# Strided attention: normalised weights, turned over by TensorE, in place of raw exponentials and a division at the exit

## Chip, cores and metric

One core of a Trainium2 chip. The metric is the device time of one execution in microseconds; a kernel's time is the median of its runs. The profile of one execution gives, beside that, the span from the first to the last instruction and what every engine did in it.

## The reference

Every query attends to the same 16 positions, every 64th of 1024. There are 8 x 12 = 96 heads with 64 dimensions, all in float32:

```python
for i in range(seq):
    attend_positions = np.arange(0, seq, stride)          # 0, 64, ..., 960
    q = Q[:, :, i:i + 1, :]
    k = K[:, :, attend_positions, :]
    v = V[:, :, attend_positions, :]
    scores = np.einsum('bhqd,bhkd->bhqk', q, k) * scale   # scale = 1/8
    weights = np.exp(scores - np.max(scores, axis=-1, keepdims=True))
    weights = weights / (np.sum(weights, axis=-1, keepdims=True) + 1e-10)
    result[:, :, i, :] = np.einsum('bhqk,bhkd->bhqd', weights, v)[:, :, 0, :]
```

## The kernel before, in words

The 96 heads are 24 groups (`NG`) of 4 heads. A group's queries are 1 MB of float32 and lie in SBUF as 128 partitions of 2048 elements: a partition holds 32 queries of one head, 64 dimensions each. Ten buffers `qn` take the loads, eight `out_sb` the stores. All DMAs go through the SP queue: the first ten loads of Q (and K's and V's rows) at the start, then one load and one store a group. The last groups' stores go in pairs, and the very last store has its own place at the end.

For each group the steps are these:

- `cast` (L326): Q to bf16 in `qb`, one half by ScalarE (ACT), one half by GpSimd (POOL).
- `transpose` (L337): VectorE (DVE) turns 32x32 blocks of pairs of bf16 (as int32), so that the dimensions lie on partitions, in `qt`.
- `scores` (L343, products in L463 to 477): TensorE (PE) multiplies four times, 512 columns wide, the keys `k_t` as the stationary operand and the queries as the moving one. The scores come out with the keys (head and position) on partitions and the queries along the columns, in one PSUM bank `sc`.
- two exponentials by ScalarE (L353), 64 partitions each, from PSUM straight into the block matrix `w_all`. No maximum is subtracted.
- `outputs` (L367): eight products `w x v_all`, 260 columns wide, in blocks of 3, 2 and 3, into two PSUM tiles `o` of three banks. `v_all` carries the values in a block diagonal (made by POOL, `values`, L316) and four columns of ones, whose products are the sums of the weights.
- the exit: for each block VectorE takes the reciprocal of the sums (L453); for the first two blocks it multiplies the outputs by it from PSUM into `out_sb` (L459); the third block is copied by ScalarE (L383) and multiplied by POOL in SBUF (L385).

The order on each engine is written out by hand. `Program.op` records the operations in order with what they read and write, `plan` works out which waits are needed, and `emit` writes the instructions; every engine carries out its own in the order recorded. PE and VectorE run loops (`pe_stream`, `dve_stream`: four groups a turn on PE, eight on VectorE); ScalarE, POOL and SP are written out straight. Semaphores named "gates" (`turned`, `raised`, `scaled`, `copied`, ...) tell the loops how far the other engines are. Scores run one group ahead of the outputs, casts and transposes two or three.

Of the kernel before, what the change touches and what calls it, by code (L numbers as in the profile page):

```python
# [42 lines left out]
class Program:  # L43
# [13 lines left out]
    def op(self, engine, fn, reads=(), writes=(), after=(), lane=None, gate=None, gates=(), looped=False, last=False):  # L57
# [12 lines left out]
        for k in writes:  # L70
# [3 lines left out]
            gate=gate, gates=gates, last=last, looped=looped or engine == "PE",  # L74
# [3 lines left out]
    def plan(self):  # L78
# [12 lines left out]
        for i, o in enumerate(self.ops):  # L91
# [4 lines left out]
            for d in sorted(o["deps"], reverse=True):  # L96
                p = self.ops[d]
                if p["lane"] == e and (e == "PE" or d not in o["own"]):
                    continue
                if known[e].get(p["lane"], -1) >= d:  # L100
                    continue
                assert not o["looped"], ("needs more gates", i, e, d, p["lane"])
                while d is not None and self.ops[d]["gate"]:
                    later = (j for j in range(d + 1, i) if self.ops[j]["lane"] == p["lane"])
                    d = next(later, None)
                if d is None:
                    d = self.ops.index(p)
                    gate_waits.append((p["gate"], carriers[p["gate"]].index(d) + 1))
                else:
                    waits.append(d)  # L110
                learn(e, d)
# [22 lines left out]
    def emit(self, loops):  # L134
# [8 lines left out]
        with self.tc.tile_critical(no_gpsimd_drain=True):  # L143
            for e in ("ACT", "DVE", "POOL"):
                engines[e].addr_align(128, max_nops=0)
            for o in self.ops:
                if o["looped"]:
                    continue
                for gate, n in o["gates"]:
                    engines[o["engine"]].wait_ge(gates[gate], n)  # L150
# [8 lines left out]
            nc.sync.wait_ge(sems["POOL"], counts["POOL"])  # L159
            for loop in loops:  # L160
                loop(sems, gates)
# [5 lines left out]
def kernel(  # L167
# [19 lines left out]
    KW = P + NK  # L187
    TURN = 4
    ROUNDS = 8
    assert B * H == NG * HG and S == 1024 and D == 64 and NK == 16 and NG % TURN == NG % ROUNDS == 0  # L190
# [6 lines left out]
    edge = sb.tile([P, 32], FP32, name="edge")  # L197
    k_raw = sb.tile([P, NC, D], FP32, name="k_raw")
    v_raw = sb.tile([P, NC, D], FP32, name="v_raw")
    k_bf = sb.tile([P, NC, D], BF16, name="k_bf")  # L200
    identity = sb.tile([P, P], BF16, name="identity")
    qn = [sb.tile([P, 32 * D], FP32, name=f"qn{i}") for i in range(QBUFS)]
    qb = [sb.tile([P, 32 * D], BF16, name=f"qb{i}") for i in range(2)]
    out_all = [sb.tile([P, 2, 4, 8, D], FP32, name=f"out_sb{i}") for i in range(OBUFS // 2)]
    out_sb = [out_all[i // 2][:, i % 2] for i in range(OBUFS)]
    qt = [sb.tile([P, 32 * D], BF16, name=f"qt{i}") for i in range(2)]
    rec = [sb.tile([P, 8, 4], FP32, name=f"rec{i}") for i in range(2)]
    w_all = sb.tile([P, 2, 8, P], BF16, name="w_all")
    v_all = sb.tile([P, 4, 4 * D + 4], BF16, name="v_all")
    w_bufs, v_bufs = [w_all[:, i] for i in range(2)], [v_all[:, i] for i in range(4)]  # L210
    k_t = sb.tile([P, NG + 1, 2, KW], BF16, name="k_t")
    k_r = sb.tile([P, NC, D], BF16, name="k_r")
    v_bf = sb.tile([P, NC, D], BF16, name="v_bf")
    v_rep = sb.tile([P, NC, 2, D], BF16, name="v_rep")
    perm_v = sb.tile([P, 2, 2, 2, 2, NK], BF16, name="perm_v")
    s_sel = sb.tile([P, 4], BF16, name="s_sel")
    mask = sb.tile([P, 4, D], BF16, name="mask")
    sc_ps = [ps.tile([P, 512], FP32, name=f"sc{i}") for i in range(2)]
    o_ps = [ps.tile([P, 3, 512], FP32, name=f"o{i}") for i in range(2)]
# [4 lines left out]
    blocks = ((0, 3), (3, 2), (5, 3))  # L224
# [19 lines left out]

    op("POOL", lambda: nc.gpsimd.memset(identity, 0.0), writes=["identity"])
# [5 lines left out]
    for c in range(2):  # L251
        for a in range(2):
            op("POOL", lambda c=c, a=a: nc.gpsimd.tensor_copy(
                out=perm_v[:, c, a],
                in_=id_v[:, c, :, a].unsqueeze(2).to_broadcast([P, 2, 2, NK]),
            ), reads=["identity"], writes=[f"perm{c}{a}"])
    op("DVE", lambda: nc.vector.memset(k_t, 0.0),  # L257
       writes=[f"k_t{m}{c}{s}" for m in range(2) for c in range(2) for s in range(4)],
       gate="scaled")
    op("DVE", lambda: nc.vector.memset(w_all, 0.0),  # L260
       writes=[f"w{i}{a}" for i in range(2) for a in range(2)], gate="scaled")
# [5 lines left out]
        out=v_all[:, :, 4 * D :], in_=s_sel.unsqueeze(1).to_broadcast([P, 4, 4])  # L267
    ), reads=["s_sel"], writes=["ones"])
    op("POOL", lambda: nc.gpsimd.tensor_copy(
        out=mask, in_=s_sel.unsqueeze(2).to_broadcast([P, 4, D])  # L270
    ), reads=["s_sel"], writes=["mask"])

# [11 lines left out]
    def keys(m, c, s):  # L284
        part = halves[m]
        src, dst, col = 32 * (2 * c + s % 2), 32 * (2 * (s % 2) + s // 2), NK + 32 * s
        e, fn = (
            ("DVE", nc.vector.tensor_copy) if m else
            ("POOL", nc.gpsimd.tensor_copy) if s >= 2 else ("ACT", nc.scalar.copy)
        )  # L290
        op(e, lambda: fn(  # L291
# [3 lines left out]
            )[:, s // 2],  # L295
        ), reads=[f"k_r{m}"] + ["mask", "turn"] * (e == "POOL"),
           writes=[f"k_t{m}{c}{s}"] + ["turn"] * (e == "POOL"), gate="copied" if (m, c, s) == (0, 1, 1) else None)

    def value_sums(n):
        rows = o_ps[n][:, 0:2, 0 : NC // 2 * D].rearrange("p c (n d) -> p c n d", d=D)  # L300
        for c in range(2):
            r = nc.tensor.matmul(  # L302
                rows[:, c], lhsT=perm_v[:, c].rearrange("p a b e k -> p (a b e k)"),
                rhs=v_bf[:, 6 * n : 6 * n + 6], start=True, stop=True,
            )
        return r

    def value_rows(n):
        op("PE", None, reads=["v_bf"] + [f"perm{c}{a}" for c in range(2) for a in range(2)],
           writes=[f"o{n}"], gates=[("masked", 1)], gate="out")  # L310
        rows = o_ps[n][:, 0:2, 0 : NC // 2 * D].rearrange("p c (n d) -> p c n d", d=D)
        op("DVE", lambda: nc.vector.tensor_copy(  # L312
            out=v_rep[:, 6 * n : 6 * n + 6].rearrange("p n c d -> p c n d"), in_=rows
        ), reads=[f"o{n}"], writes=[f"v_rep{n}"], gates=[("out", n + 1)])

    def values(g):  # L316
        v = v_bufs[g % 4]
        op("POOL", lambda: nc.gpsimd.tensor_tensor(  # L318
            out=v[:, 0 : 4 * D].rearrange("p (s d) -> p s d", s=4), in0=mask,
            in1=v_rep[:, g // 2, g % 2].unsqueeze(1).to_broadcast([P, 4, D]),  # L320
            op=ALU.mult,
        ), reads=["mask", "v_rep0", "v_rep1"], writes=[f"v{g % 4}"], gate="masked")

    half = 16 * D

    def cast(g):  # L326
        q, b = qn[g % QBUFS], qb[g % 2]
        op("ACT", lambda: nc.scalar.copy(b[:, half:], q[:, half:]),  # L328
           reads=[f"qn{g % QBUFS}1"], writes=[f"qb{g % 2}1"])
        op("POOL", lambda: nc.gpsimd.tensor_copy(out=b[:, 0:half], in_=q[:, 0:half]),  # L330
           reads=[f"qn{g % QBUFS}0"] + [f"qb{g % 2}1"] * (g >= 2) + ["turn"] * (g < 2),
           writes=[f"qb{g % 2}0"] + ["turn"] * (g < 2), gate="cast")

    def turn_over(g):
        return nc.vector.transpose(qt[g % 2].bitcast(I32), qb[g % 2].bitcast(I32))  # L335

    def transpose(g):  # L337
        k_in = {0: "00", 1: "01"}.get(g)
        op("DVE", lambda: turn_over(g),
           reads=[f"qb{g % 2}0", f"qb{g % 2}1"] + [f"k_t{k_in}{s}" for s in range(4) if k_in],  # L340
           writes=[f"qt{g % 2}"], gate="turned", gates=[("cast", g + 1)], looped=g >= 2)

    def scores(g):  # L343
        s = g % 2
        op("PE", None,
           reads=[f"qt{g % 2}"] + [f"k_t{int(min(g, NG - 1) >= 8)}{g % 2}{i}" for i in range(4)],
           writes=[f"sc{s}0", f"sc{s}1"], gates=[("turned", g + 1)])
        if g == NG:
            return
        sc, w = sc_ps[s], w_bufs[g % 2]  # L350
        for a in range(2):
            wa = w[64 * a : 64 * a + 64]
            op("ACT", lambda a=a, wa=wa: nc.scalar.activation(  # L353
                out=_ap_with(wa, [wa.ap[0], [P, 8], [1, 2], [2, 32]], extra_offset=64 * a),
                in_=sc[64 * a : 64 * a + 64].rearrange("p (t x q) -> p t x q", t=8, x=2),
                func=AF.Exp, bias=0.0, scale=scale,
            ), reads=[f"sc{s}{a}"], writes=[f"w{g % 2}{a}"], gate="raised" if a else None,
               after=[stored[g - OBUFS]] if a and g >= OBUFS else [])

    def parts(g, c):  # L360
        i0, n = blocks[c]
        r = rec[g % 2][:, i0 : i0 + n]
        o = o_ps[(3 * g + c) % 2][:, 0:n, 0 : 4 * D].rearrange("p i (s d) -> p i s d", s=4)
        to = out_sb[g % OBUFS][:, :, i0 : i0 + n].rearrange("p s i d -> p i s d")
        return r, o, to, r.unsqueeze(3).to_broadcast([P, n, 4, D])

# [180 lines left out]
```

## Time and profile before

| what | value |
|---|---|
| time, median of 3 runs | 127.56 us (127.49, 127.56, 128.0) |
| span of the profiled execution | 125.9 us; its own time is not listed apart, the three runs are 1.6 to 2.1 us longer than this span |
| busy: PE, DVE, ACT, POOL | 66.5, 90.7, 80.9, 78.2 us |
| DMA | 51.15 MB, mean 406 GB/s |
| chain that ended last | DMA 25%, PE 20%, DVE 20%, ACT 13%, POOL 8% |

A row of the profile names the line of the kernel, the engine and the operation, what is written and read, the shape and the count; behind the first bar stand the busy time in us and the mean duration of one in ns, behind the second the idle time of the engine just before, and what ended it. PEld is the loading of TensorE's stationary operand. PEclk is the granted clock of TensorE, in tenths of full speed for each of 40 slices of the span.

### The profile page before, as it was taken

What the parts mean: (1) busy time and instruction counts of PE and PEld (TensorE: products, weight loads), DVE (VectorE), ACT (ScalarE), POOL (GpSimd) and SP (SyncE); (2) the same over time, 40 slices, a digit from 0 to 9 for tenths busy, and PEclk for the clock granted to TensorE, in tenths of its full rate; (3) what the DMA queues carried; (4) which work ended last, traced back from release to release, by engine and by line L of the source; (5) the groups of instructions that cost most, each with busy time, mean ns of one, the idle gap of its engine ahead of it and who ended that gap; (6) DMA issues with size and microseconds to landing.
All of it is one profiled execution on the core that took longest, in us unless ns stands there. A gap on an engine that the chain in (4) does not pass through costs nothing.

```text
span 125.9 us, 1283 instructions
## 1 busy us (share of the span) xinstructions
PE 66.5 (53%) x296; PEld 29.7 (24%) x296; DVE 90.7 (72%) x161; ACT 80.9 (64%) x103; POOL 78.2 (62%) x89
## 2 busy tenths in 40 slices
PE   0005472887777796466555666478664663840000
PEld 0001130343333333233212333233332320410000
DVE  2996457978669669989997999966999794970000
ACT  4270943686966786989999799968698655711000
POOL 4074247387865956988999699986699851534000
PEclk9999999755685559999999999955999999755555
DMA  1999989899899999899798998999998999999991
GB/s 43 423 312 479 479 354 500 354 479 448 344 417 458 403 435 495 359 474 469 338 515 354 411 515 341 430 458 398 440 482 364 450 427 422 422 422 422 424 424 70
DMA packets 7140, 51.15 MB, mean 406 GB/s; under 512 B 3808, under 2 KB 3808, under 8 KB 3808
## 3 DMA queue, kind: packets, MB, share of 16 engines
q1 hardware_dynamic: 7136, 51.12, 96.9%
q14 instruction: 4, 0.03, 0.1%
HBM read 25.95 MB, written 25.17 MB: 406 GB/s over the span
## 4 chain that ended last, share of the span: by engine, by line
DMA 25%; PE 20%; DVE 20%; ACT 13%; POOL 8%; issue 4%; SPq 1%; ACTq 0%; DVEq 0%; POOLq 0%
DMA out_dram<-out_sb 18%; DVE out_sb L459 12%; PE o L497 10%; PE sc L469 10%; DMA qn<-in_Q_dram 7%; ACT w_all L353 5%; ACT out_sb L383 4%; DVE qt L335 4%; POOL out_sb L385 4%; ACT qb L328 3%; DVE rec L453 3%; POOL qb L330 2%; DVE v_rep L312 1%; POOL v_all L318 1%; SPq L236 1%
## 5 line engine op out<-in xcount | busy, mean ns | idle before, releaser
L497 PE MATMUL o<-v_all,w_all 128*128 128x260 bf16 x192 | 38.8, 327 | 28.5 <-DVE out_sb L459 24.2
L385 POOL TENSOR_TENSOR out_sb<-out_sb,rec 128x768 f32<-128x768 f32 x24 | 35.3, 1472 | 25.3 <-ACT out_sb L383 25.3
L469 PE MATMUL sc<-qt,k_t 128*128 128x512 bf16 x100 | 33.3, 464 | 16.5 <-DVE qt L335 12.3
L459 DVE TENSOR_TENSOR out_sb<-o,rec 128x768 f32<-128x768 f32 (+1 forms) x48 | 39.6, 825 | 1.6
L353 ACT ACTIVATE w_all<-sc 64x512 bf16<-64x512 f32 x48 | 35.2, 733 | 7.3 <-DMA out_dram<-out_sb 3.5
L335 DVE STREAM_TRANSPOSE qt<-qb 128x1024 int32<-128x1024 int32 x26 | 31.6, 1214 | 3.6 <-POOL qb L330 3.5
L497 PEld LDWEIGHTS o<-v_all,w_all 128*128 128x128 bf16 x192 | 18.3, 112 | 52.4 <-DVE out_sb L459 33.0
L383 ACT COPY out_sb<-o 128x768 f32<-128x768 f32 x24 | 19.2, 799 | 16.5 <-DVE rec L453 16.2
L328 ACT CAST qb<-qn 128x1024 bf16<-128x1024 f32 x24 | 25.0, 1045 | 4.3 <-DVE v_rep L312 1.4
L330 POOL CAST qb<-qn 128x1024 bf16<-128x1024 f32 x24 | 24.9, 1039 | 1.9 <-DMA qn<-in_Q_dram 1.7
L453 DVE RECIPROCAL rec<-o 128x12 f32<-128x12 f32 (+1 forms) x72 | 15.4, 213 | 11.7 <-PE o L497 10.9
L318 POOL TENSOR_TENSOR v_all<-mask,v_rep 128x256 bf16<-128x256 bf16 x24 | 16.0, 670 | 4.2 <-DVE v_rep L312 4.1
L469 PEld LDWEIGHTS sc<-qt,k_t 128*128 (+1 forms) x100 | 10.9, 110 | 27.7 <-issue 11.7
L257 DVE MEMSET k_t<- 128x3600 uint32 x1 | 3.1, 3058 | 2.3 <-issue 2.3
L312 DVE CAST v_rep<-o 128x768 bf16<-128x768 f32 x2 | 1.9, 939 | 2.6 <-PE o L302 2.6
L291 DVE COPY k_t<-k_r 32x256 bf16<-32x256 bf16 x8 | 3.2, 395 | 0.1
L277 ACT CAST k_bf<-k_raw 128x256 bf16<-128x256 f32 (+1 forms) x2 | 0.9, 508 | 2.6 <-DMA k_raw<-in_K_dram 2.6
L266 POOL COPY v_all<-s_sel 128x16 bf16<-128x16 bf16 x1 | 0.2, 197 | 3.7 <-DVE s_sel L262 3.7
L277 ACT ACT_TABLE_LOAD x1 | 1.3, 1283 | 1.3 <-SPq L143 1.3
L302 PE MATMUL o<-v_bf,perm_v 128*128 128x384 bf16 x4 | 1.5, 520 | 1.0 <-POOL v_bf L416 1.0
L291 ACT COPY k_t<-k_r 32x128 bf16<-32x128 bf16 x4 | 1.2, 295 | 0.8 <-DVE k_r L279 0.7
L291 POOL COPY k_t<-k_r 32x128 bf16<-32x128 bf16 x4 | 1.2, 290 | 0.3
(13 smaller groups left out, 5.1 us busy)
## 6 DMA issues: line engine op xcount, KB each, us to landing
qn<-in_Q_dram SPq DMA_DIRECT2D x24, 1024.0 KB, 15.4
out_dram<-out_sb SPq DMA_DIRECT2D x16, 1024.0 KB, 14.0
out_dram<-out_sb SPq DMA_DIRECT2D x4, 2048.0 KB, 17.4
k_raw<-in_K_dram SPq DMA_DIRECT2D x1, 384.0 KB, 4.2
v_raw<-in_V_dram SPq DMA_DIRECT2D x1, 384.0 KB, 6.7
```

The lines of the kernel that those rows point to most:

```text
L291: op(e, lambda: fn(k_t[dst : dst + 32, 2 * part.start + c : 2 * part.stop : 2, :, col : col + NK], k_r[src : src + 32, part].rearrange("p ...
L318: op("POOL", lambda: nc.gpsimd.tensor_tensor(out=v[:, 0 : 4 * D].rearrange("p (s d) -> p s d", s=4), in0=mask, in1=v_rep[:, g // 2, g % 2] ...
L328: op("ACT", lambda: nc.scalar.copy(b[:, half:], q[:, half:]), reads=[f"qn{g % QBUFS}1"], writes=[f"qb{g % 2}1"])
L330: op("POOL", lambda: nc.gpsimd.tensor_copy(out=b[:, 0:half], in_=q[:, 0:half]), reads=[f"qn{g % QBUFS}0"] + [f"qb{g % 2}1"] * (g >= 2) + [ ...
L335: return nc.vector.transpose(qt[g % 2].bitcast(I32), qb[g % 2].bitcast(I32))
L353: op("ACT", lambda a=a, wa=wa: nc.scalar.activation(out=_ap_with(wa, [wa.ap[0], [P, 8], [1, 2], [2, 32]], extra_offset=64 * a), in_=sc[64 ...
L383: op("ACT", lambda: nc.scalar.copy(to, o), reads=[o_key], writes=[to_key, f"copy{g}"], after=[sums])
L385: op("POOL", lambda: nc.gpsimd.tensor_tensor(out=to, in0=to, in1=by, op=ALU.mult), reads=[to_key, r_key], writes=[to_key], last=g == NG - 1)
L453: sums = dve.reciprocal(r, o_ps[(3 * j + c) % 2][:, 0 : blocks[c][1], 4 * D : 4 * D + 4])
L459: dve.tensor_tensor(out=to, in0=o, in1=by, op=ALU.mult).then_inc(gates["scaled"], 1)
L469: r = pe.matmul(sc_ps[g % 2], lhsT=k_t[:, k, f, NK * (1 - e) : NK * (1 - e) + P], rhs=_ap_with(qt[g % 2], [qt[g % 2].ap[0], [D, 8], [16 * ...
L497: r = pe.matmul(o_ps[(3 * j + c) % 2][:, i, 0 : 4 * D + 4], lhsT=w_bufs[j % 2][:, i0 + i], rhs=v_bufs[j % 4], start=True, stop=True,)
```

## The change

The scores change sides. The queries in `qt` become the stationary operand (16 loads of 128 columns a group) and the keys the moving one (64 columns), so that the scores stand with 128 queries on partitions and 32 x 16 (query block and head part, position) along the columns of one PSUM bank. For this the transpose stores its words with a stride.

Then the softmax is made in full before the outputs:

- `largest`: VectorE takes the maximum over 16 positions from PSUM and subtracts it from the scores (PSUM to SBUF, 512 elements, `low`, one buffer).
- `raise_`: one exponential by ScalarE, 128 partitions x 512, SBUF to SBUF, float32.
- `sums`: VectorE adds over 16 positions and takes the reciprocal (32 elements).
- `weights`: POOL multiplies the exponentials by the reciprocal, into bf16 `wt`.
- `turn`: TensorE turns `wt` over, four 128 x 128 products with the identity, into a bf16 PSUM tile `tp`.
- `spread`: ScalarE copies `tp` in two halves of 64 partitions into the block matrix `wb`.
- `outputs`: eight products of 256 columns, in two halves of two PSUM banks each; there are no ones in `v_all` any more, and `v_all` is kept for all 24 groups, made for two groups at a time by POOL.
- `evict`: ScalarE copies each half, 128 x 1024 float32, from PSUM to `out_sb`; VectorE and POOL have no part in the exit. The evictions of a group are recorded in the next group's turn, one ahead of its spread copies and one behind.

From the fourth group on the cast is POOL's alone, 128 x 2048 at once. Scores and transposes now run two groups ahead, casts three. PE's loop has two groups a turn and leaves the last two groups to straight code; VectorE's loop is gone and its instructions are written out. The second half of the keys' copies moves into groups 1 to 4. The load of group g+9 and the store of group g-1 are issued in the turn of group g, behind the second eviction of g-1.

The core of the diff:

```diff
+    def score_products(g, k):
+        for i in range(8):
+            for f in range(2):
+                r = nc.tensor.matmul(
+                    _ap_with(
+                        sc_ps[g % 2], [sc_ps[g % 2].ap[0], [64, 2], [1, 32]],
+                        extra_offset=128 * (i // 2) + 32 * (i % 2),
+                    ),
+                    lhsT=_ap_with(qt[g % 2], [qt[g % 2].ap[0], [2, P]], extra_offset=2 * P * i + f),
+                    rhs=k_t[:, k, f], start=f == 0, stop=f == 1,
+                )
+        return r
...
+    def largest(g):
+        s = sc_ps[g % 2].rearrange("p (t k) -> p t k", k=NK)
+        m = top[g % 2]
+        op("DVE", lambda: nc.vector.tensor_reduce(
+            out=m, in_=s, op=ALU.max, axis=mybir.AxisListType.X,
+        ), reads=[f"sc{g % 2}"], writes=[f"top{g % 2}"])
+        op("DVE", lambda: nc.vector.tensor_tensor(
+            out=low, in0=s, in1=m.unsqueeze(2).to_broadcast([P, 32, NK]), op=ALU.subtract,
+        ), reads=[f"sc{g % 2}", f"top{g % 2}"], writes=["low"])
+
+    def raise_(g):
+        op("ACT", lambda: nc.scalar.activation(
+            out=ex[g % 2], in_=low, func=AF.Exp, bias=0.0, scale=scale,
+        ), reads=["low"], writes=[f"ex{g % 2}"])
+
+    def sums(g):
+        t, r = total[g % 2], rec[g % 2]
+        op("DVE", lambda: nc.vector.tensor_reduce(
+            out=t, in_=ex[g % 2], op=ALU.add, axis=mybir.AxisListType.X,
+        ), reads=[f"ex{g % 2}"], writes=[f"total{g % 2}"])
+        op("DVE", lambda: nc.vector.reciprocal(r, t),
+           reads=[f"total{g % 2}"], writes=[f"rec{g % 2}"])
+
+    def weights(g):
+        op("POOL", lambda: nc.gpsimd.tensor_tensor(
+            out=wt[g % 2], in0=ex[g % 2],
+            in1=rec[g % 2].unsqueeze(2).to_broadcast([P, 32, NK]), op=ALU.mult,
+        ), reads=[f"ex{g % 2}", f"rec{g % 2}"], writes=[f"wt{g % 2}"], gate="weighted")
+
+    def turn_products(g):
+        for c in range(4):
+            r = nc.tensor.transpose(
+                tp_ps[:, 2 * c : 2 * c + 2].rearrange("p a b -> p (a b)"),
+                wt[g % 2][:, 8 * c : 8 * c + 8].rearrange("p t k -> p (t k)"), identity,
             )
         return r
...
+    def spread(g):
         for a in range(2):
+            rows = slice(64 * a, 64 * a + 64)
+            op("ACT", lambda rows=rows: nc.scalar.copy(wb[g % 2][rows, :, rows], tp_ps[rows]),
+               reads=[f"tp{a}"], writes=[f"wb{g % 2}{a}"], gate="copied" if a else None)
...
+    def evict(g, n):
+        to = out_sb[g % OBUFS].rearrange("p b (c x) d -> p c b (x d)", c=4)[:, 2 * n : 2 * n + 2]
+        op("ACT", lambda: nc.scalar.copy(
+            to, o_ps[:, 2 * n : 2 * n + 2].rearrange("p c (b x) -> p c b x", b=2),
+        ), reads=[f"o{n}"], writes=[f"out{g % OBUFS}{n}"],
+           after=[stored[g - OBUFS]] if g >= OBUFS else [], last=g == NG - 1 and n == 1)
+        if n and g + 1 < NG:
+            op("ACT", lambda: nc.scalar.nop(), reads=[f"out{g % OBUFS}{n}"], gate="freed")
...
     for g in range(NG):
+        looped = g < looped_groups
+        largest(g)
+        raise_(g)
+        if g + 2 < NG:
+            transpose(g + 2)
+        sums(g)
         if g + 3 < NG:
+            cast(g + 3, False)
...
+        weights(g)
+        if g % 2 == 0 and g // 2 + 1 < NC:
+            values(g // 2 + 1)
         if g + 2 < NG:
+            scores(g + 2, looped)
+        if g >= 1:
+            evict(g - 1, 0)
+        turn(g, looped)
+        spread(g)
+        if g >= 1:
+            evict(g - 1, 1)
...
+        outputs(g, 0, looped)
+        outputs(g, 1, looped)
+    evict(NG - 1, 0)
+    evict(NG - 1, 1)
...
+        with pe.Fori(0, looped_groups // TURN) as turn_:
             for j in range(TURN):
+                pe.wait_ge(gates["turned"], j + 3)
+                score_products(j, turn_ * TURN + (j + 2)).then_inc(done, 1)
+                pe.wait_ge(gates["weighted"], j + 1)
+                turn_products(j).then_inc(done, 1)
+                pe.wait_ge(gates["copied"], j + 1)
+                output_products(j, turn_ * TURN + j, 0).then_inc(done, 1)
+                pe.wait_ge(gates["freed"], j + 1)
+                output_products(j, turn_ * TURN + j, 1).then_inc(done, 1)
```

More of the change, by code (lines that the diff above doesn't have):

```diff
@@ L266 @@
     op("POOL", lambda: nc.gpsimd.tensor_copy(
-        out=v_all[:, :, 4 * D :], in_=s_sel.unsqueeze(1).to_broadcast([P, 4, 4])
-    ), reads=["s_sel"], writes=["ones"])
-    op("POOL", lambda: nc.gpsimd.tensor_copy(
         out=mask, in_=s_sel.unsqueeze(2).to_broadcast([P, 4, D])
     ), reads=["s_sel"], writes=["mask"])
+    op("DVE", lambda: nc.vector.memset(wb_all, 0.0),
+       writes=[f"wb{i}{a}" for i in range(2) for a in range(2)])
     halves = (slice(0, 4), slice(4, NC))
@@ L282, in key_rows, with keys @@
         ), reads=[f"k_bf{m}"], writes=[f"k_r{m}"])
-    def keys(m, c, s):
+    def keys(m, c, h, engine):
         part = halves[m]
[L286 to L291, printed above, removed]
+        src, dst = 32 * (2 * c + h // 2), 32 * h
+        col = 32 * (h % 2) + NK * (h // 2)
+        fn = {
+            "DVE": nc.vector.tensor_copy, "POOL": nc.gpsimd.tensor_copy, "ACT": nc.scalar.copy,
+        }[engine]
+        op(engine, lambda: fn(
             k_t[dst : dst + 32, 2 * part.start + c : 2 * part.stop : 2, :, col : col + NK],
@@ L308, in value_rows @@
[L308 to L350, printed above, removed]
-        for a in range(2):
[L352 to L358, printed above, removed]
@@ new lines, in keys, with value_rows, products @@
+            )[:, h % 2],
+        ), reads=[f"k_r{m}"], writes=[f"k_t{m}{c}{h}"])
+    def value_rows(n):
+        rows = o_ps[:, 2 * n : 2 * n + 2, 0 : NC // 2 * D].rearrange("p c (n d) -> p c n d", d=D)
+        def products():
+            for c in range(2):
+                r = nc.tensor.matmul(
+                    rows[:, c], lhsT=perm_v[:, c].rearrange("p a i b k -> p (a i b k)"),
+                    rhs=v_bf[:, 6 * n : 6 * n + 6], start=True, stop=True,
+                )
+            return r
+        op("PE", products, reads=["v_bf"] + [f"perm{c}{a}" for c in range(2) for a in range(2)],
+           writes=[f"o{n}"], gates=[("values", 1)])
+        op("DVE", lambda: nc.vector.tensor_copy(
+            out=v_rep[:, 6 * n : 6 * n + 6].rearrange("p n c d -> p c n d"), in_=rows
+        ), reads=[f"o{n}"], writes=[f"v_rep{n}"])
@@ new lines, in values, with cast @@
+    def values(n):
+        op("POOL", lambda: nc.gpsimd.tensor_tensor(
+            out=v_all[:, 2 * n : 2 * n + 2].rearrange("p c (s d) -> p c s d", s=4),
+            in0=mask.unsqueeze(1).to_broadcast([P, 2, 4, D]),
+            in1=v_rep[:, n].unsqueeze(2).to_broadcast([P, 2, 4, D]),
+            op=ALU.mult,
+        ), reads=["mask", f"v_rep{n // 6}"], writes=[f"v{n}"])
+    half = 16 * D
+    def cast(g, shared):
+        q, b = qn[g % QBUFS], qb[g % 2]
+        if shared:
+            op("ACT", lambda: nc.scalar.copy(b[:, half:], q[:, half:]),
+               reads=[f"qn{g % QBUFS}1"], writes=[f"qb{g % 2}1"])
+            op("POOL", lambda: nc.gpsimd.tensor_copy(out=b[:, 0:half], in_=q[:, 0:half]),
+               reads=[f"qn{g % QBUFS}0"], writes=[f"qb{g % 2}0"])
+        else:
+            op("POOL", lambda: nc.gpsimd.tensor_copy(out=b, in_=q),
+               reads=[f"qn{g % QBUFS}{h}" for h in range(2)],
+               writes=[f"qb{g % 2}{h}" for h in range(2)])
@@ L398, in store @@
         sent = op("SP", lambda: send(g, n), lane=f"out{g % OBUFS}",
-                  reads=[f"out{i % OBUFS}{c}" for i in both for c in range(3)])
+                  reads=[f"out{i % OBUFS}{c}" for i in both for c in range(2)])
         stored.update((i, sent) for i in both)
@@ L403 @@
     key_rows(1)
-    for s in range(4):
-        keys(0, 0, s)
-    for s in range(4):
-        keys(1, 0, s)
-    cast(0)
-    transpose(0)
-    for s in range(4):
-        keys(0, 1, s)
-    for s in range(4):
-        keys(1, 1, s)
-    scores(0)
-    cast(1)
+    for h in range(4):
+        keys(0, 0, h, "DVE" if h >= 2 else "ACT")
+    cast(0, True)
+    transpose(0)
+    for h in range(4):
+        keys(0, 1, h, "DVE" if h >= 2 else "ACT")
+    scores(0, False)
+    cast(1, True)
+    transpose(1)
@@ L416 @@
+    scores(1, False)
     op("POOL", lambda: nc.gpsimd.tensor_copy(out=v_bf, in_=v_raw), reads=["v_raw"],
-       writes=["v_bf"], gate="masked")
+       writes=["v_bf"], gate="values")
     value_rows(0)
-    transpose(1)
     value_rows(1)
+    cast(2, True)
     values(0)
-    values(1)
-    cast(2)
+    looped_groups = NG - TURN
     for g in range(NG):
-        transpose(g + 2)
-        if g + 3 < NG:
-            cast(g + 3)
-        elif g + 1 < NG:
-            op("POOL", lambda: nc.gpsimd.nop(), reads=[f"out{(g - 1) % OBUFS}2"], gate="cast")
-        if g + 2 < NG:
-            values(g + 2)
-        scores(g + 1)
-        for c in range(3):
-            outputs(g, c)
-        if g + 1 < NG:
-            op("ACT", lambda: nc.scalar.nop(), reads=[f"copy{g}"], gate="copied")
-        if g + QBUFS < NG:
-            load(g + QBUFS)
-        if g < NG - QBUFS or g == NG - 2:
-            store(g, 1)
-        elif g % 2 and g < NG - 2:
-            store(g - 1, 2)
```

203 lines of the change are left out of this document (82 added, 121 removed).

## The prediction, made before the changed kernel ran

> **What bounds the kernel now.** I read the page first (engines, slices, queues), then the granted clock in the slices, then the chain of waits and the timeline of the loop, and last the groups by shape for the prices.
>
> ```profile
> span 125.9 us, 1283 instructions
> PE 66.5 (53%) x296; PEld 29.7 (24%) x296; DVE 90.7 (72%) x161; ACT 80.9 (64%) x103; POOL 78.2 (62%) x89
> PEclk9999999755685559999999999955999999755555
> q1 hardware_dynamic: 7136, 51.12, 96.9%
> ```
>
> The queue is busy for 96.9% of the span and no engine for more than 72%. The 51.12 MB are 24 loads and 24 stores, so a group needs 2.1 MB. At the 429 GB/s of the second window below that is 4.9 us a group. The engines turn a group round in less: in the next rows the same matmuls of two neighbouring groups start 4.50 us apart.
>
> ```profile
> 43.40 0.83 PE L497 MATMUL o<-v_all,w_all 128*128 128x260 bf16 x3 [0.89 <-DVE out_sb L459]
> 47.90 0.51 PE L497 MATMUL o<-v_all,w_all 128*128 128x260 bf16 x3 [0.89 <-DVE out_sb L459]
> ...
> 113.71 1.47 POOL L385 TENSOR_TENSOR out_sb<-out_sb,rec 128x768 f32<-128x768 f32 x1 [2.52 <-ACT out_sb L383]
> 115.75 0.54 SPq L34 DMA_DIRECT2D out_dram<-out_sb  x1
> ```
>
> The last arithmetic ends at 115.2, the last store is issued at 115.75, and the rest of the 125.9 us is queued stores landing. So the transfers bound this kernel, and the engines run about 10 us ahead of them. The change can gain almost nothing; it loses once the engines need more than 4.9 us a group. Span against median: 127.56 - 125.9 = 1.66 us lie outside the span, and I add that at the end. The three runs differ by 0.4%, so about 0.5% is what a measurement can tell.
>
> **The change, part by part.** Order matters more than work here. Per group ScalarE now queues, strictly in this order: exp(g); the eviction of the first half of g-1; two spread copies of g; the eviction of the second half of g-1; a marker; then exp(g+1). The spread copies of g need PE's turn of g, which needs POOL's weights, which need VectorE's sums and reciprocal, which need exp(g). ScalarE therefore cannot start exp(g+1) until a round trip over four engines has come back. In the kernel before no such loop exists: the unnormalised exp feeds the outputs directly, and the division comes at the exit. The prices come from the groups by shape (behind the first bar: busy us and the mean ns of one; behind the second: idle time before it):
>
> ```profile
> L353 ACT ACTIVATE w_all<-sc 64x512 bf16<-64x512 f32 x48 | 35.2, 733 | 7.3 <-DMA out_dram<-out_sb 3.5 <-PE sc L469 3.3
> L262 DVE TENSOR_REDUCE s_sel<-identity 128x4 bf16<-128x128 bf16 x1 | 0.2, 228 | 0.0
> L459 DVE TENSOR_TENSOR out_sb<-o,rec 128x512 f32<-128x512 f32 x24 | 16.6, 692 | 0.8
> L459 DVE TENSOR_TENSOR out_sb<-o,rec 128x768 f32<-128x768 f32 x24 | 23.0, 957 | 0.8
> L453 DVE RECIPROCAL rec<-o 128x12 f32<-128x12 f32 x48 | 10.6, 221 | 11.7 <-PE o L497 10.9
> L385 POOL TENSOR_TENSOR out_sb<-out_sb,rec 128x768 f32<-128x768 f32 x24 | 35.3, 1472 | 25.3 <-ACT out_sb L383 25.3
> L318 POOL TENSOR_TENSOR v_all<-mask,v_rep 128x256 bf16<-128x256 bf16 x24 | 16.0, 670 | 4.2 <-DVE v_rep L312 4.1
> L383 ACT COPY out_sb<-o 128x768 f32<-128x768 f32 x24 | 19.2, 799 | 16.5 <-DVE rec L453 16.2
> L328 ACT CAST qb<-qn 128x1024 bf16<-128x1024 f32 x24 | 25.0, 1045 | 4.3 <-DVE v_rep L312 1.4 <-DMA qn<-in_Q_dram 0.8
> L277 ACT CAST k_bf<-k_raw 128x512 bf16<-128x512 f32 x1 | 0.6, 612 | 0.0
> L330 POOL CAST qb<-qn 128x1024 bf16<-128x1024 f32 x24 | 24.9, 1039 | 1.9 <-DMA qn<-in_Q_dram 1.7
> L335 DVE STREAM_TRANSPOSE qt<-qb 128x1024 int32<-128x1024 int32 x26 | 31.6, 1214 | 3.6 <-POOL qb L330 3.5
> ```
>
> And a stretch of the chain of waits (start us, us, what) for what lies between two instructions and between neighbours on ScalarE:
>
> ```profile
> 56.93 0.02 issue
> 56.95 0.02 ACTq L436
> 56.96 0.07 issue
> 57.03 1.04 ACT qb L328
> 58.07 0.64 ACT w_all L353
> 58.71 0.01 issue
> 58.73 0.73 ACT w_all L353
> ```
>
> Link by link, with PE at full clock:
> - exp, 512 elements a partition: 0.73, the L353 row. One such pass replaces two.
> - sums, a reduction of 512: the L262 row has 228 ns for 128 elements; 384 more at the 1.035 ns by which the 768- and 512-element multiplies differ, (957 - 692)/256, make 0.63; the 512-element multiply, 0.69, is the other end. I take 0.65.
> - reciprocal of 32: 221 ns for 12 and twenty more at 1.035 make 0.24; all of it in proportion would be 0.59. I take 0.25, since 221 for so few is nearly all fixed.
> - weights on POOL, 512 f32: 1472 x 512/768 = 0.98; between the 256- and 768-element rows by a straight line, 1.07. I take 1.03. The Trainium skill (GPSIMD Engine Reference, section on elementwise side-by-side accounting) gives about 2.6 cycles an element at 1.2 GHz for two inputs, an estimate of 1.11 here; that would add 0.08 to the link and 1.8 us to the total, and the measured row is the lower and decides.
> - turn, four 128-wide products with four weight loads: three 260-column products took 0.51 at full clock and 0.83 at half (rows at 47.90 and 43.40), so 0.107 each, 0.21 at half clock, and 0.19 fixed. Four loads of 0.077 (below) and the 0.19 make 0.50.
> - two spread copies of 512 from PSUM: ScalarE's casts step by (1045 - 612)/512 = 0.846 ns an element, so 0.799 - 256 x 0.846 = 0.58 each; the chain lets a neighbour start 0.64 after the start of a 0.73 exp, an overlap of 0.09, so 1.0 until the next copy starts.
> - eviction of 1024: 0.799 + 256 x 0.846 = 1.01. The first half of g-1 lies in ScalarE's wait and costs nothing; the second is on the loop.
> - hops, from the chain of waits: 0.02 to 0.07 for each of seven, 0.09 for the marker: 0.33.
>
> Sum: 0.73 + 0.65 + 0.25 + 1.03 + 0.50 + 1.0 + 1.01 + 0.33 = 5.50 us a group, against 4.9 of DMA. ScalarE works 0.73 + 1.0 + 1.01 + 1.0 + 0.09 = 3.8 of these and waits the rest.
>
> What lies beside the loop. VectorE's maximum 0.65, subtraction 0.69 and transpose 1.21 for the next groups make 2.55 after a reciprocal. The next exp, which reads the subtraction, starts 3.8 after that reciprocal, and the next sums, which stand behind the transpose, 4.5 after it. So 1.9 are left: the transpose with its new strided store may take twice as long before it is felt. The second half of the keys moves into groups 1 to 4, on ScalarE behind exp, inside its wait, and on VectorE within those 1.9. POOL's whole cast (at most 2 x 1.04) and every second group's values (up to 1.4, twice the L318 row) make 3.5 between two weights; these are 4.4 apart. Q loads are issued six groups ahead, over 30 us, and need 15.4 (row below); the stores, moved behind the second eviction, only meet a queue with room. The cast halves that leave ScalarE and VectorE's and POOL's scaling of the outputs go.
>
> PE has a loop of its own. Its queue holds, in order, scores(g+2), turn(g), outputs of both halves. The second half waits for the marker, so scores stand behind it and the next turn behind the scores. For the clock, the core's mean, windows of the loop (PE busy, PEld, DVE, ACT, POOL, PEclk, DMA share, GB/s), then a wait, weight loads and the loads of Q:
>
> ```profile
> core 0: 125.9 us, clock 0.823
> ...
> 37.80:47.20 9.40, 7.44 (x25) 3.27 (x24) 7.02 (x14) 6.81 (x10) 6.57 (x8) 0.50 1.02 431
> 54.00:72.00 18.00, 10.73 (x61) 5.07 (x60) 16.76 (x32) 16.03 (x21) 15.36 (x16) 1.00 1.01 429
> ...
> PE sc L469 <- issue: 4.2, 5, 0.9
> ...
> 44.45 0.15 PEld L469 LDWEIGHTS sc<-qt,k_t 128*128 x1 [0.28 <-issue]
> 51.09 0.23 PEld L497 LDWEIGHTS o<-v_all,w_all 128*128 128x128 bf16 x3 [1.22 <-DVE out_sb L459]
> ...
> qn<-in_Q_dram SPq DMA_DIRECT2D x24, 1024.0 KB, 15.4
> ```
>
> A weight load takes 0.23/3 = 0.077 at clock 1.00 (row at 51.09) and 0.15 at 0.50 (row at 44.45). Scores are now 16 loads with only 64 columns each, so the loads set their pace: 16 x 0.077 = 1.2 warm, 2.4 cold (1.7 if loads overlap by a third; 3.2 if each product's 64 columns, 0.053 at half clock, come on top). The loop's jump back costs up to 0.9 and now comes every second group, 0.42 each. From the start of the spread copies, PE's loop is 2.01 (spread, eviction) + 0.1 + four 256-column products (0.43 warm, 0.85 cold) + 0.42 + scores + turn (0.50, cold 0.75): 4.7 warm, hidden behind the 5.50; 6.55 cold, which then decides (5.9 to 7.4). In the trace clocks under 1 fill about a third of the loop: the mean of 0.823 is 35% at 0.5. PE is to be busy 3.0 of 5.5 us (eight products 0.86, scores 1.2, turn 0.5, fixed ends 0.4), near the 10.73 of 18 now, so I keep that share: 0.65 x 5.50 + 0.35 x 6.55 = 5.87 us.
>
> Ends. These rows of the start carry over:
>
> ```profile
> 1.46 0.73 SPq L34 DMA_DIRECT2D qn<-in_Q_dram  x1
> ...
> 7.62 1.04 ACT L328 CAST qb<-qn 128x1024 bf16<-128x1024 f32 x1 [0.20 <-DMA qn<-in_Q_dram]
> ...
> 11.49 1.07 POOL L330 CAST qb<-qn 128x1024 bf16<-128x1024 f32 x1 [1.74 <-DMA qn<-in_Q_dram]
> ...
> 14.25 0.96 DVE L312 CAST v_rep<-o 128x768 bf16<-128x768 f32 x1 [2.58 <-PE o L302]
> ```
>
> The second cast and the value rows stay at 11.49 and 14.25. Two value copies (1.9), maximum and subtraction bring exp(0) to 17.5. With the transpose of 1.2 inside, group 0's round trip without evictions takes 5.0: exp(1) at 22.5. Then 22 cycles. After exp(23): 4.5 to the end of its spread, 0.95 and 0.95 for two evictions, 1.0 for the last, then the final store. The first load needed 6.2 us from issue to its cast, behind the load of the keys; 5.1 is my estimate for a store with part of another ahead. Together 12.5. Span 22.5 + 22 x 5.87 + 12.5 = 164.1; with 1.66, 165.8, so 166.
>
> **Rivals.**
> - The clock stays full: 22 x 5.50 + 35 + 1.66 = 157.7 us. For it: 54 to 72 us ran at 1.00 with PE 60% busy, like the forecast cycle. Against: 37.8 to 47.2 stayed at 0.50 with PE 79% busy and its gaps at 0.9. The Trainium skill (TensorE: Matmul & The Clock Gate, section on why this matters for your kernels) says that only idle gaps above about 3 us throttle again, which would give this case since no gap in my cycle exceeds 1.5; the trace disagrees at 37.8 to 47.2.
> - The clock stays low and PE's loop decides: 22 x 6.55 + 35 + 1.66 = 180.8 (166 to 199 by the bounds of the scores). For it: many short products; against: two thirds of the loop now run near 1.00.
> - Not slower: ScalarE's waits are filled, because links overlap that I add. Then its own 3.8 us of work rule, 35 + 84 = 119, under the DMA floor, and the time stays 126 to 128.5. It decides below 4.1 us a cycle (35 + 22 x 4.1 = 125.2), so 1.4 us would have to leave a chain in which each link reads what the one before wrote. The order of ScalarE's queue speaks against it.
>
> **Numbers.** Forecast, mixed clock: 0.47, 161 to 172. Full clock 0.26, low clock 0.21, not slower 0.06. 154 to 181 leaves out the last, half of the low clock and 0.03 besides, 0.19 in all. Of the not-slower case 0.03 is faster by over 0.5%, 0.03 is the same; slower 0.94.
>
> **What would show it.** Right: on ScalarE a long idle before the first spread copy, released by PE's turn; exps 5.5 to 6.6 us apart, wider where the granted clock is 0.5; the queue's share down to about three quarters; the chain of waits running through exp, sums, POOL weights, turn and spread. In cold stretches the turn follows the scores without a gap. Wrong: exps under 5 us apart, a queue still above 95%, or VectorE without idle time before the sums.

## The result, and the profile after

| | before | after |
|---|---|---|
| median | 127.53 us (127.45 to 128.00, 4 runs) | 168.74 us (168.39 to 169.07, 4 runs) |
| ratio | | 1.321 (95% interval 1.317 to 1.325) |
| span of the profiled execution (its time) | 125.9 us | 166.6 us (168.39) |
| DMA queue's share of the span | 96.9% | 78.2% |

The forecast was 166, from 154 to 181. One run of the kernel with both edits below, 136.41 us, is 1.9% above that kernel's fastest, is counted as slow and is left out of its time and ratio. From the page of the changed kernel (engines, granted clock by slices, DMA queue):

```profile
span 166.6 us, 2003 instructions
PE 84.9 (51%) x676; PEld 51.9 (31%) x676; DVE 90.0 (54%) x135; ACT 97.2 (58%) x134; POOL 83.4 (50%) x72
PEclk9999999659555567555555555555558555765555
q1 hardware_dynamic: 7136, 51.12, 78.2%
```

VectorE's busy time is what it was (90.7 before), TensorE's is 18 us more, ScalarE's 16 and POOL's 5, yet none of them is busy for more than 58% of the span and the queue has fallen to 78%. Neither the work of one engine nor the transfers fill the time. The engines wait for one another, and the list of waits (us in total, times, longest) names a ring:

```profile
POOL wt L389 <- DVE rec L385: 61.8, 24, 4.8
DVE total L382 <- ACT ex L376: 54.1, 23, 3.6
ACT wb_all L409 <- PE tp L396: 47.7, 24, 3.3
...
PE tp L396 <- POOL wt L389: 22.0, 24, 1.9
```

Once per group POOL waits for VectorE, VectorE for ScalarE, ScalarE for TensorE and TensorE for POOL. What closes the ring is ScalarE's own queue. In the chain that ended last (start us, us, what), one round reads:

```profile
82.71 0.64 ACT ex L376
83.35 0.02 issue
83.37 0.70 DVE total L382
84.07 0.02 issue
84.09 0.36 DVE rec L385
84.46 0.07 issue
84.53 1.07 POOL wt L389
85.59 0.05 issue
85.64 0.62 PE tp L396 x4
86.26 0.02 issue
86.29 0.58 ACT wb_all L409
86.86 0.01 issue
86.88 0.58 ACT wb_all L409
87.46 0.02 issue
87.48 1.02 ACT out_sb L431
88.50 0.02 issue
88.52 0.02 ACTq L436
88.54 0.07 issue
88.61 0.64 ACT ex L376
```

(ACTq L436 is the marker, a `nop` that counts the gate `freed`.) From exp to exp it is 5.90 us, against the 4.50 from group to group of the prediction's rows of the kernel before. The input of the exp at 88.61 had been ready since 85.72, as the timeline shows; it stood behind two spread copies and an eviction:

```profile
85.03 0.69 DVE L371 TENSOR_TENSOR low<-sc,top 128x512 f32<-128x512 f32 x1
```

The groups by shape give the means of three links over the run:

```profile
L409 ACT COPY wb_all<-tp 64x512 bf16<-64x512 bf16 x48 | 27.8, 579 | 48.0 <-PE tp L396 47.7
L376 ACT ACTIVATE ex<-low 128x512 f32<-128x512 f32 x24 | 15.1, 629 | 6.4 <-DVE low L371 3.8
L385 DVE RECIPROCAL rec<-total 128x32 f32<-128x32 f32 x24 | 8.5, 353 | 0.8
```

The whole time follows: the first full round begins at 23.76, the last exp at 153.09, so 22 rounds of 5.88, and 13.5 us to the end.

### The profile page after: what moved, and what is told of

Read it like the earlier page. It is cut to its first block, busy times and chain, and to the rows that moved or that the text cites. A ratio compares the mean times of both kernels' runs of the same rounds, so it can differ in the third digit from the quotient of the medians.

```text
span 166.6 us, 2003 instructions
## 1 busy us (share of the span) xinstructions
PE 84.9 (51%) x676; PEld 51.9 (31%) x676; DVE 90.0 (54%) x135; ACT 97.2 (58%) x134; POOL 83.4 (50%) x72
## 3 DMA queue, kind: packets, MB, share of 16 engines
q1 hardware_dynamic: 7136, 51.12, 78.2%
## 4 chain that ended last, share of the span: by engine, by line
ACT 40%; DVE 18%; POOL 16%; PE 11%; issue 5%; DMA 5%; SPq 1%; ACTq 0%; DVEq 0%
ACT wb_all L409 17%; POOL wt L389 16%; ACT out_sb L431 14%; DVE total L382 10%; ACT ex L376 9%; PE tp L396 8%; DVE rec L385 5%; DMA qn<-in_Q_dram 5%; DVE qt L342 1%; PE o L415 1%; DVE v_rep L313 1%; ACT qb L330 1%; PE sc L350 1%; SPq L241 1%; SPq L34 0%
## 5 line engine op out<-in xcount | busy, mean ns | idle before, releaser
L415 PE MATMUL o<-v_all,wb_all 128*128 (+1 forms) x192 | 46.2, 397 | 34.4 <-ACT wb_all L409 32.4
L389 POOL TENSOR_TENSOR wt<-ex,rec 128x512 bf16<-128x512 f32 x24 | 25.7, 1073 | 61.8 <-DVE rec L385 61.8
L409 ACT COPY wb_all<-tp 64x512 bf16<-64x512 bf16 x48 | 27.8, 579 | 48.0 <-PE tp L396 47.7
L431 ACT COPY out_sb<-o 128x1024 f32<-128x1024 f32 x48 | 48.2, 1004 | 1.0 <-PE o L415 0.3
L335 POOL CAST qb<-qn 128x2048 bf16<-128x2048 f32 x21 | 39.7, 1888 | 0.0
L415 PEld LDWEIGHTS o<-v_all,wb_all 128*128 128x128 bf16 x192 | 20.2, 127 | 55.0 <-issue 35.2
L350 PE MATMUL sc<-k_t,qt 128*128 (+1 forms) x384 | 25.9, 242 | 18.8 <-DVE qt L342 16.6
L350 PEld LDWEIGHTS sc<-k_t,qt 128*128 128x128 bf16 x384 | 23.5, 130 | 25.8 <-DVE qt L342 12.9
L332 POOL CAST qb<-qn 128x1024 bf16<-128x1024 f32 x3 | 3.1, 1040 | 7.2 <-DMA qn<-in_Q_dram 7.2
L330 ACT CAST qb<-qn 128x1024 bf16<-128x1024 f32 x3 | 3.1, 1044 | 4.6 <-DMA qn<-in_Q_dram 4.6
```

The source lines that it names most:

```text
L335: op("POOL", lambda: nc.gpsimd.tensor_copy(out=b, in_=q), reads=[f"qn{g % QBUFS}{h}" for h in range(2)], writes=[f"qb{g % 2}{h}" for h in ...
L350: r = nc.tensor.matmul(_ap_with(sc_ps[g % 2], [sc_ps[g % 2].ap[0], [64, 2], [1, 32]], extra_offset=128 * (i // 2) + 32 * (i % 2),), lhsT=_ ...
L389: op("POOL", lambda: nc.gpsimd.tensor_tensor(out=wt[g % 2], in0=ex[g % 2], in1=rec[g % 2].unsqueeze(2).to_broadcast([P, 32, NK]), op=ALU.mult,
L409: op("ACT", lambda rows=rows: nc.scalar.copy(wb[g % 2][rows, :, rows], tp_ps[rows]), reads=[f"tp{a}"], writes=[f"wb{g % 2}{a}"], gate="cop ...
L415: r = nc.tensor.matmul(_ap_with(o_ps, [o_ps.ap[0], [128, 2], [256, 2], [1, D]], extra_offset=512 * c + D * u,), lhsT=wb[g % 2][:, 2 * c + ...
L431: op("ACT", lambda: nc.scalar.copy(to, o_ps[:, 2 * n : 2 * n + 2].rearrange("p c (b x) -> p c b x", b=2),), reads=[f"o{n}"], writes=[f"out ...
```

## The experiments

The theory: the ring through ScalarE's queue sets the cycle. The rivals: a ring through TensorE's queue (scores and outputs ahead of the next turn), and the plain amount of added work.

**The eviction taken out of the ring.** Both evictions of g-1 ahead of the spread copies of g:

```diff
         if g >= 1:
             evict(g - 1, 0)
-        turn(g, looped)
-        spread(g)
-        if g >= 1:
             evict(g - 1, 1)
             if g - 1 + QBUFS < NG:
...
+        turn(g, looped)
+        spread(g)
         outputs(g, 0, looped)
```

> Both evictions of group g-1 stand ahead of the spread copies of g on ScalarE, inside its wait for the turn, instead of one ahead and one behind. If the loop through ScalarE's queue sets the cycle (5.90 us: exp 0.64, sums 0.70, reciprocal 0.36, weights 1.07, turn 0.62, spread 1.17, eviction 1.02, hops 0.33), the eviction and its marker, 1.13, leave it: cycle 4.8 to 4.9, about what the transfers need, and a time of 143 to 148 us. If PE's order (scores and outputs ahead of the next turn) or the amount of work sets it: 166 to 170.

142.8 us (ratio to before 1.118, 1.113 to 1.123), 0.2 below the first theory's figures and 26 us less than the changed kernel with the same instructions. In its chain the rounds are 4.6 to 4.8 us, 1.1 to 1.3 less than 5.90, where 1.13 was priced; the low end has a turn at full clock (0.41). Two rows that follow each other as exps:

```profile
76.13 0.64 ACT ex L376
...
80.69 0.64 ACT ex L376
```

The chain still runs through exp, sums, reciprocal, weights, turn and spread. The shorter time alone does not separate the two rings, since the eviction stood on TensorE's too, as the runs below show; the next edit leaves TensorE's order as it is.

**The exp taken out of the ring.** `largest(g + 1)` and `raise_(g + 1)` are recorded behind the weights of g, ahead of the evictions and spread copies:

```diff
-        largest(g)
-        raise_(g)
+        if g == 0:
+            largest(0)
+            raise_(0)
...
+        if g + 1 < NG:
+            largest(g + 1)
+            raise_(g + 1)
         if g + 2 < NG:
             scores(g + 2, looped)
```

> Maximum, subtraction and exp of group g+1 are recorded ahead of the evictions and spread copies of g, so that no exp stands behind a spread copy any more. The work on every engine is the same. Loop theory: ScalarE is left with its own 4.0 us a group and VectorE with 3.7, both under the 4.9 of the transfers, so the cycle falls to 4.9 and the time to 127.5 to 133 us. Theory that the added work sets the time: within 3% of 168.7. PE theory: little change, 160 to 170.

144.4 us (1.133, 1.127 to 1.139): 24 us less, but 11 above the top of the first theory's figures. ScalarE's ring was gone and another showed, the one through TensorE that the prediction had priced. Its chain:

```profile
81.39 0.58 ACT wb_all L409
...
81.98 0.59 ACT wb_all L409
82.57 0.14 issue
82.71 2.03 PE o L415 x8
84.74 0.85 PE sc L350 x16
85.59 0.44 PE tp L396 x4
...
86.06 0.58 ACT wb_all L409
```

Now the turn follows the scores at once, the scores follow the outputs, and the second half of the outputs waits inside the 2.03 for the eviction (1.02) and its marker. The round is 4.67 here, and 5.11 in the next one, where the scores take 1.11 and start 0.20 late, at the loop's jump back.

**Both edits.**

> Both edits at once. Loop theory: no more than the early exp alone brings, since the transfers then set the time: within 1% of it. If it is still another 5 us or more faster, a part of the loop had survived the first edit.

135.3 us (133.8 to 135.7; ratio 1.054, 1.045 to 1.063), 9 us faster than the early exp alone, so its first branch was wrong: the transfers did not yet set the time. The eviction had been on TensorE's ring too. Without it the rounds through TensorE are 4.52 us in the chain, and others, through the evictions, 4.0.

**TensorE's ring taken apart as well.** On top of the early exp, the turn of g goes ahead of the outputs of g-1, and the spread copies of g ahead of both evictions of g-1. Beside these lines the first two groups leave PE's loop, and the turn waits by a gate for the spread copies of the group before, since both use the same PSUM tile (shortened):

```diff
-        if g >= 1:
-            evict(g - 1, 0)
         turn(g, looped)
         spread(g)
         if g >= 1:
+            outputs(g - 1, 0, looped)
+            outputs(g - 1, 1, looped)
+            evict(g - 1, 0)
             evict(g - 1, 1)
...
-        outputs(g, 0, looped)
-        outputs(g, 1, looped)
```

> On top of the early exp: PE makes the turn of g ahead of the outputs of g-1, which lag by one group, and ScalarE spreads g ahead of both evictions of g-1. The traces of the two runs with the early exp show a second loop, through PE: turn, spread, eviction or marker, outputs, scores, next turn, 4.5 to 4.9 us. This order takes it apart too. If these two loops are all that was added, only the engines' work (4.0 us a group) and the transfers are left: 127.5 to 132 us, against 135.5 with the PE loop. If the tail and the start cost more than the loop, 133 to 136.

129.9 us (1.019, 1.012 to 1.026), within the first range, and the queue's share is back at 95.9%. No work was left out: the full softmax with its maximum, turn and spread copies costs 2.3 us over the kernel before once the two rings are taken apart.

**The loads of Q issued when their cast is recorded**, four groups sooner, on top of that.

> The late outputs, with the load into each Q buffer issued as soon as its cast is recorded, four groups sooner. In the late outputs the cast waits 6.4 us in all for loads of Q, which stand in SP's order behind stores. If these waits are what is left against the kernel before (129.9 to 127.6), 127 to 128.5 us; if the transfers alone bind, unchanged within 0.7%; if loads ahead now make stores wait for their buffers, 130 to 133.

128.5 us (1.007, 1.004 to 1.010). The casts no longer wait for loads beyond the first three groups, and the span and the queue's share are nearly those of the kernel before (125.9 us, 96.9%):

```profile
span 126.6 us, 2018 instructions
...
q1 hardware_dynamic: 7136, 51.12, 96.5%
```

It does not beat 127.6: the queue has 51.12 MB to move in both.

**TensorE given more to do.** `for i in [*range(8), *range(8)]` in `score_products`, then three times eight.

> The changed kernel with its 16 score products made twice, 0.85 us more PE work a group at the pace of the trace (1.06 for 16, less 0.2 of fixed end). Loop through ScalarE: PE's own loop is 4.9 long and becomes 5.75, still under 5.90: within 1% of 168.7, or some us less if the fuller PE raises the granted clock (turn 0.41 instead of 0.62). PE theory: 22 x 0.85, 187 us.

169.8 us, 0.6% above the changed kernel, where TensorE's ring would have given 187. TensorE had room for 16 more products a round, but hardly for more: in ten of the rounds from 24 us on the chain already runs through the doubled scores (1.7 to 2.0 us).

> Score products three times, 1.7 us more. PE's loop is now 6.6 and longer than the 5.90: 22 x 0.7 more, 180 to 188 us at half clock; less where the clock is full, since the products are then half as long.

174.2 us, below the 180 to 188 at half clock. The chain shows why. Two neighbouring rounds, the first limited by TensorE, the second not:

```profile
82.31 2.67 PE sc L350 x48
84.98 0.44 PE tp L396 x4
...
89.58 1.07 POOL wt L389
...
90.70 0.41 PE tp L396 x4
```

In the first round 48 products take 2.67 and hold the turn up. In the second they take 2.02 by the timeline (granted clock 0.74 from 88.0 to 91.1) and end at 90.60, just ahead of the weights, so ScalarE's ring decides again. The 180 to 188 were for half clock throughout; 11 of the 24 turns here took 0.39 to 0.41, the length at full clock.

**The maximum left out, in three kernels.** First without maximum and subtraction; exp reads PSUM, and the transpose of g+2 moves behind the sums:

```diff
-        largest(g)
         raise_(g)
+        sums(g)
         if g + 2 < NG:
             transpose(g + 2)
-        sums(g)
```

> Leaves out the maximum and the subtraction: exp reads the scores from PSUM; the transpose of g+2 stands behind the reciprocal instead of ahead of the sums. VectorE loses 1.33 us a group. Loop theory: neither instruction is on the loop, the cycle stays at 5.9 and only the start is shorter by 1.3: 166 to 169 us. Theory that VectorE's added work costs the time: 24 x 1.33 less, 137 us.

195.1 us: less work, and 26 us slower. The move of the transpose had made a new link. The row of POOL's cast says which:

```profile
L335 POOL CAST qb<-qn 128x2048 bf16<-128x2048 f32 x21 | 39.7, 1889 | 62.3 <-DVE total L382 61.5
```

POOL's cast of g+3 needs the transpose of g+1, which counts only on TensorE's gate; the wait is put on the next counted VectorE instruction, now the sums of g. So the cast of 1.89 starts inside the ring, ahead of the weights. With the cast behind the weights:

> Again without maximum and subtraction, now with POOL's cast of g+3 recorded behind the weights of g. In the first try the cast waited for the sums of g (the transpose it waits for gives no count, so the next counted VectorE instruction stands in for it) and then held up the weights. If that alone made 195, the loop is as in the changed kernel: cycle 5.9, 165 to 169 us. If maximum and subtraction cost time themselves: 137 to 150.

187.8 us, a miss again. The cast was out, but the scores of g+2 stand ahead of the turn of g in TensorE's queue and wait for the transpose, which now comes after the reciprocal (one round of the chain):

```profile
85.73 0.35 DVE rec L385
86.09 1.11 DVE qt L342
...
87.36 1.11 PE sc L350 x16
88.48 0.44 PE tp L396 x4
```

Neither run tells what maximum and subtraction cost; both tell what it costs to move an instruction of 1.2 us behind another. The third kernel leaves all in place and drops only the maximum (`top` is set to zero once):

> Leaves out the maximum alone: VectorE subtracts a tile of zeros, every other instruction and its place as in the changed kernel. VectorE has 0.64 us a group less to do. Loop theory: the maximum is not on the loop, cycle 5.90 as before, 0.6 less at the start: 167 to 169 us. Theory that VectorE's added work costs time: 24 x 0.64 less, 153.

168.5 us, the changed kernel's time, with VectorE busy 73.4 us in place of 90.0. The maximum, 24 x 0.64 of VectorE's work, costs nothing where it stands. What the subtraction alone costs was not tried.

**A link made longer.** The reciprocal made twice:

> The reciprocal made twice, 0.37 us more on VectorE, which is idle for over 2 us a group. Loop theory: the reciprocal is on the loop, so every cycle grows by 0.37: 23 x 0.37, 177.2 us (176 to 178.5). If only busy time counted: 168.7 to 169.5.

178.1 us, 9.4 more, where 8.5 was forecast. Two rows of its chain:

```profile
88.57 0.36 DVE rec L385
88.94 0.02 issue
88.96 0.36 DVE rec L387
```

This pair is the sharpest: on one engine that idles for more than 2 us a group, 0.64 us a group taken away does nothing, and 0.38 us a group added, 24 x 0.38 = 9.1 in all, costs 9.4.

## Why the prediction was right, step by step

**The bound before.** Right: with the same transfers, three reorderings bring the same new work back to within 0.7%.

**The ring and its order.** Right, link by link; the sum was short by 0.40:

| link | forecast | measured |
|---|---|---|
| exp | 0.73 | 0.64 |
| sums | 0.65 | 0.70 |
| reciprocal | 0.25 | 0.36 |
| weights | 1.03 | 1.07 |
| turn | 0.50 | 0.62 at half clock, 0.41 at full |
| two spread copies | 1.00 | 1.16 |
| second eviction | 1.01 | 1.02 |
| hops and marker | 0.33 | 0.32 |
| sum | 5.50 | 5.90 |

The largest misses have reasons in rows. The reciprocal had been taken as nearly all fixed; 353 ns for 32 against 221 for 12 is 6.6 ns an element. The turn came out at both clocks: 0.41 at full, where 0.50 was forecast, and 0.62 at half. The spread copies are 0.58 each as priced, but they start 0.59 apart and do not overlap, though an exp and its neighbour did before, and so do two evictions (1.93 for two of 1.015, in the run with both evictions first). Why those overlap and these do not is open. The exp took 629 ns where 733 was priced. That it reads SBUF in place of PSUM is not the reason: in the first kernel without the maximum it read the scores from PSUM and took 597. The old pass also wrote bf16 into 64 partitions of a block matrix; which of this costs the 0.10 is open. The weights took 1.07 for the forecast's 1.03. The Trainium skill (GPSIMD Engine Reference, section on elementwise side-by-side accounting) gives a rate from which the estimate was 1.11.

**TensorE's ring.** This step failed: "6.55 cold, which then decides", and with it the mean 0.65 x 5.50 + 0.35 x 6.55 = 5.87. Half clock was more frequent than assumed: 18 of the 22 rounds have a turn of 0.61 to 0.62 us, where a share of 0.35 was forecast. By the forecast's own prices that share would have made 0.18 x 5.50 + 0.82 x 6.55 = 6.36 a round, and yet TensorE's ring did not decide. Two rows of the changed kernel's timeline, and one of its groups by shape:

```profile
83.52 1.06 PE L350 MATMUL sc<-k_t,qt 128*128 x16
...
85.64 0.61 PE L396 MATMUL tp<-identity,wt 128*128 128x128 bf16 x4 [1.06 <-POOL wt L389]
...
L350 PEld LDWEIGHTS sc<-k_t,qt 128*128 128x128 bf16 x384 | 23.5, 130 | 25.8 <-DVE qt L342 12.9 <-issue 11.3
```

TensorE has idled for 1.06 before the turn and waits for POOL, not for its own scores. The term that was mis-sized is the scores at half clock: 2.4 forecast, with 1.7 as the lower end, and 1.06 measured with the fixed end, 0.85 where the turn follows at once. 0.85 is 0.053 for each product together with its weight load, what the prediction reckoned for the 64 columns alone. The loads are listed at 130 ns each, but 384 of them fill 23.5 us and not 384 x 0.130 = 49.9: they overlap, and the duration of one was not the pace of many. The turn, 0.75 forecast at half clock, takes 0.44 behind the scores. With these the ring is 4.67 to 5.11 (the early exp), under 5.90. So 5.87 met 5.90 by two errors that cancel: 0.37 too much for TensorE, and 0.40 too little in ScalarE's ring. Of the 0.40, 0.21 is the turn at half clock, which the 5.50 left out; rounds with a turn of 0.41 are 5.69. The interval held for the right bound, the number partly by luck.

**Beside the ring.** The transpose, the casts, the keys, the loads and the stores were to cost nothing, and no wait of theirs is on the chain of a round. The two failed tries without the maximum show how narrow that is: it held for the places they stood in.

**Ends.** Forecast 22.5 and 12.5, measured 23.8 and 13.5.

**Rivals.** "The clock stays full" fell: 18 of 22 rounds had a turn at half clock. In the changed kernel the turn at 38.78 took 0.41 and the one at 44.56 took 0.62, so the clock fell between them, and TensorE had no idle gap above 1.4 us there (1.9 is the longest in any round). The Trainium skill (TensorE: Matmul & The Clock Gate, section on why this matters for your kernels) advises to leave no idle gaps above about 3 us between bursts of matmuls, so that the throughput does not drop. Here, as in the kernel before, that was not enough. "The clock stays low and PE's loop decides" had the clock nearly right and the price wrong. "Not slower" did not come about in this order, and its condition, ScalarE's waits filled, is what the late outputs brought about.

**Signs named.** A long idle before the first spread copy (47.7 us in 24 waits, 2.0 each), exps 5.9 apart and a queue at 78%: right. "In cold stretches the turn follows the scores without a gap": wrong, as above.

## What to carry to other kernels

Before costing a change by busy time, write down each engine's queue over one round and look for a ring: an instruction of the next round that stands behind one that needs a result of this round. The ring's length is a sum of durations and hops that can be read from single rows, and its cure is order: recording the next round's first step ahead of this round's last, and the same on the second ring, took 39 us off without removing any work. When a ring is cut, the next longest appears, so price all of them, and check that a moved instruction has not joined one.

## What the runs showed of the hardware that was not expected

The mean granted clock listed for a run is not always the speed at which TensorE ran. The changed kernel is listed at 0.633. The line of the first kernel without the maximum, and a turn in its chain:

```profile
core 0: 193.3 us, clock 1.000
...
76.45 0.62 PE tp L396 x4
```

By that mean the kernel ran at full clock throughout. Yet all 24 of its turns took 0.61 to 0.62 us, the length at half clock, as did 20 of 24 in the changed kernel, and its page has no PEclk row at all. The second kernel without the maximum is the same: listed at 1.000, with no PEclk row and all 24 turns at that length. In the changed kernel the first 24.5 us are listed at 1.00 as well, while the turn at 21.92 took 0.61. So 1.00 can stand where no clock was recorded, and the duration of an instruction that comes back in every round is the safer gauge. The prediction's share of 35% was read from such a mean: in the kernel before, the stretch from 3 to 23 us is listed at 1.00, but the four score products at 16.65 took 1.88, against 1.06 at 55.51.

By that gauge the clock does not follow how busy TensorE is. The turn had its full-clock length (0.39 to 0.41) in none of 24 groups where TensorE was busy for 46% of the span, in 15 at 48% (late outputs), in 4 at 51% (changed kernel) and in 11 at 59% (scores three times). Four runs of the changed kernel, with listed means from 0.633 to 0.77, took 168.39 to 169.07 us: of the clock only the turn's 0.2 us a round is on the ring. What sets the clock stays open.
